# Neighbourhood attention in blocks of 8 columns on quarters of the matrix array, with a joined first load and a residual that waits in PSUM

## The chip, the cores and the metric

One core of one Trainium2 chip runs the whole layer. The metric is the device time of one execution in microseconds, as the median of several runs. The core has a matrix engine (TensorE, PE in the profile; its weight loads are PEld), a vector engine (VectorE, DVE), a scalar engine (ScalarE, ACT), GpSimd (POOL) and SyncE (SP), which here issues transfers. A suffix q (SPq, ACTq) marks an engine's queue of instructions that are not work of its own, such as issues of transfers.

## The reference, cut to what matters

One encoder layer in float32 on 512 tokens (8 rows of 64 columns) of 2048 features:

```python
xn = rms_norm(x, attn_norm_g)
u_val, u_gate, q, k, v = split(xn @ w_in)          # 1024 columns each
y_conv = silu(layer_norm(depthwise_conv31(u_val * sigmoid(u_gate))))
y_na = neighborhood_attention(q, k, v, rpb)        # 16 heads of 64
x = x + concat(rms_norm(y_conv), rms_norm(y_na)) @ w_out
up = depthwise_conv3(rms_norm(x) @ w_up)           # 2 x 5632 columns
gate, val = split(up)
x = x + (silu(gate) * val) @ w_down
out = rms_norm(x)

# neighborhood_attention, for the token in grid row r, grid column c:
#   the window is all 8 grid rows, and 16 grid columns from
#   clip(c - 8, 0, 48);  p = softmax(q.k / 8 + bias[head, dr, dc]);  out = p.v
```

With 8 grid rows the window takes in every row, so that only the columns limit it: a query in column c sees keys of 16 columns about c.

## The kernel before

**Numbers.** Large products are made of two or three matmuls of a reduced float32 type (fp32r): an operand is split into a high part, rounded by ScalarE (`whi`, `xh`), and a low remainder, by VectorE (`wlo`, `xl`). `group` multiplies a 128x1024 unit of weights in this way: 8 high weights with the high and the low activations (L153, L154), then 8 low weights with the high ones (L156), 24 matmuls of 512 columns. Attention alone, and the transposes, work in plain float32.

**Stages.** 16 steps in the order `ORDER = "aaaqqaqaaaqqaqqq"` make the input projection: a step "a" is a gate and a value projection of 128 convolution channels (`glu`, two projections), a step "q" is q, k and v of a pair of heads (`qkv`, three projections). A projection is two units. Then the output projection in two halves, the up projection (44 blocks of seven products, a fast matrix multiplication of two by two blocks with seven products), the down projection of the same kind (`product2`, seven products of 22 units), and the last norm. TensorE's order is that of the program as the tile framework schedules it by priorities; `pin` keeps a group of instructions in program order.

**Attention between the projections.** After each unit, `tick` takes one step of the first generator in `steps`, with its instructions placed behind the unit just multiplied. `attend` is such a generator: loads of the bias tables, then the turned values and the scores with their softmax, three or four ticks of pause, then the transposes of the probabilities (`turn`, L521) with their copies out of PSUM (`turned_p`, L529), then the values (`values`, L538) with their copy (L571) into the split operand of the output projection.

The 64 grid columns are cut into 4 blocks of 16 columns; a block is 128 queries (8 rows x 16 columns). The two edge blocks have 192 keys, the two middle blocks 256, in groups of 8 columns (64 keys). A score matmul (L495) has 64 rows of the array, the features of one head, and 128 columns, the queries; the two heads of a pair lie on the two halves of the rows. For keys that do not start at an even group, `qkv` makes a second copy `ks` of the keys on ScalarE with the groups exchanged in pairs, and `turned_v` arranges the turned values twice (`edge`, `vt`, five copies on ScalarE). A value matmul has 128 keys on the rows and the 64 features of one head on half of the columns, and moves 128 queries; the two heads lie on the two halves of the columns. PSUM tiles: `sc` (two banks) holds edge scores and later edge transposes, two `tr` banks the middle ones, `po` (one bank) the turned values and later the result of the values. Two statistics of the convolution's norms (`root_steps`, the matmul `st<-dg` L255) use `sc` as well.

**The start.** `w_0` holds the weights of the first gate and the first value projection, interleaved by the 16 rows of 128 features. The first rows come as separate loads: the norm's scales `g1` and three weight pieces on ScalarE's queue, x on SyncE's. `first_glu` multiplies a row of x with two weight blocks as soon as it is there: six matmuls a row (L369, L373). 11 matmuls of ones (`WARM`, L124) run ahead of it. The next projections follow with whole units.

**The end.** The last product, `product2(5, a, False)`, starts four PSUM banks anew; its last four units are multiplied bank by bank (`TAIL`), so that each bank's end can be worked on beside the next. In `ready` VectorE adds the bank to the partial sum `x` of the other products (L935), ScalarE squares that with a sum (L937), VectorE multiplies with the last norm's gain (L939, or together with the scale, L965, for the last block of a row); `write` makes the scale of the norm from the sums, multiplies and stores (L953 to L969), the last block of a row first.

Of the kernel before, what the change touches and what calls it, by code (L numbers as in the profile page):

```python
# [16 lines left out]
P = 128  # L17
# [19 lines left out]
BLK = 16  # L37
NB = GW // BLK
HG = 8
EDGE, MID = (0, 3), (1, 2)  # L40
KEYS = ((0, 0, 3 * DH), (1, 0, 4 * DH), (1, 2 * DH, 4 * DH), (0, 5 * DH, 3 * DH))
ATEDGE = ((0, 0), (1, 1)), ((1, 2), (2, 3))
ATMID = ((0, 0), (1, 1)), ((2, 1), (3, 2))
# [8 lines left out]
WARM = 11  # L52
# [26 lines left out]
def layer(ctx: ExitStack, tc: tile.TileContext, xT, xn, w_0, w_in, w_out, w_up, w_down, par, tab, g3, out):  # L79
# [26 lines left out]
    nc.scalar.dma_start(g1, par[:, :KD])  # L106
    cuts = (0, 1, 2, 4, 8, 12, 16)
    first = []
    for k0, k1 in zip(cuts[:3], cuts[1:4]):
        first.append(t2("we")[:, :2 * (k1 - k0) * P])  # L110
        nc.scalar.dma_start(first[-1], w_0[:, 2 * k0 * P:2 * k1 * P])
# [159 lines left out]
    def split_x(k, x):  # L271
        h, l = t2("xh", F32R), t2("xl", F32R)
        pin(nc.scalar.activation(h, x, AF.Copy, scale=g1[:, k:k + 1]))
        pin(nc.vector.scalar_tensor_tensor(l, x, g1[:, k:k + 1], h.bitcast(F32), op0=ALU.mult, op1=ALU.subtract))
        xs.append((h, l))

    def piece(raw, k0, k1):
        if k1 - k0 > 2:
            raw, i = raw_unit(w_0[:, 2 * k0 * P:2 * k1 * P], 2 * (k1 - k0) * P)
            pin(i)  # L280
            w = parts(raw, 2 * (k1 - k0) * P)
        else:
            w = t2("weh", F32R)[:, :2 * (k1 - k0) * P], t2("wel", F32R)[:, :2 * (k1 - k0) * P]
            w += nc.scalar.activation(w[0], raw, AF.Copy), nc.vector.tensor_sub(w[1], raw, w[0].bitcast(F32))
        pin(w[2])
        pin(w[3])
        return k0, k1, w[0], w[1]

    pieces, early = [], []
    for k in range(2):  # L290
        x = t2("x")
        pin(nc.sync.dma_start(x, xT[0][:, k * S:(k + 1) * S]))
        split_x(k, x)
        pieces.append(piece(first[k], k, k + 1))
    for p, at in ((1, 2), (2, 3), (3, 0), (4, 4), (5, 0), (6, 5), (7, 0)):
# [4 lines left out]
        if at:  # L300
            pieces.append(piece(first[2] if at == 2 else None, cuts[at], cuts[at + 1]))
    squares = sm.tile([P, S // P, 2], F32, tag="ss", name="ss")
    for u in range(2):
        raw, i = raw_unit(w_in[NC_ + 1, :, u * U * P:(u + 1) * U * P], U * P)
        pin(i)
        for t in range(2 * u, 2 * u + 2):
            for i in range(2):
                x = t4([P, D // 2], "xn")
                pin(nc.sync.dma_start(x, xn[t * P:(t + 1) * P, i * D // 2:(i + 1) * D // 2]))
                if t == 2 * u and i == 0:  # L310
                    w = parts(raw, U * P)
                    pin(w[2])
                    pin(w[3])
                    early.append(w[:2])
                pin(nc.scalar.activation(x, x, AF.Square, accum_out=squares[:, t, i:i + 1]))
    last = pin(nc.sync.dma_start(prm, par))
    for i in range(6):
        plan.append(lambda i=i: early[i - 4] if i > 3 else None)
# [6 lines left out]
    del plan[6:12]  # L325
# [5 lines left out]
    def stats1():  # L331
        for _ in range(3):
            yield
# [19 lines left out]
    ys, ypair = [], []  # L353

    def glu(i):
        pg, pv = project(NC_ + i), project(i)

        late.append(lambda: gated(i, pg, pv))

    def first_glu():  # L360
        two = [psa.tile([P, S], F32, tag="tr", name="pj", bufs=2) for _ in range(2)]
        for n, (k0, k1, hi, lo) in enumerate(pieces):
            if n > 1:
                weights()
            for k in range(k0, k1):
                for x in range(2):
                    for i, ps in enumerate(two):
                        o = (2 * (k - k0) + i) * P
                        nc.tensor.matmul(ps, hi[:, o:o + P], xs[k][x], start=k == x == 0, stop=False)  # L369
            for k in range(k0, k1):  # L370
                for i, ps in enumerate(two):
                    o = (2 * (k - k0) + i) * P
                    m = nc.tensor.matmul(ps, lo[:, o:o + P], xs[k][0], start=False, stop=k == KD - 1)  # L373
            if n > 1:
                tick(m)
        late.append(lambda: gated(0, *two))
# [63 lines left out]
    def grid(t, c0, w):  # L440
        return t.rearrange("p (r c) -> p r c", c=GW)[:, :, c0:c0 + w]

    def qkv(p):
        got = []
        for j, nm in enumerate("qkv"):
            ps = project(2 * NC_ + j * NP_ + p)
            if nm == "q":

                t = t2(nm)
                by = "p (r b c) -> p r b c"  # L450
                nc.vector.tensor_mul(t.rearrange("p (b r c) -> p r b c", b=NB, r=WH),
                                     ps.rearrange(by, b=NB, r=WH), rstd[0].rearrange(by, b=NB, r=WH))
            else:

                t = t2(nm)
                by = "p (r g c) -> p r g c"
                nc.vector.tensor_mul(t.rearrange("p (g r c) -> p r g c", g=2 * NB, r=WH),
# [620 lines left out]
```

## Time and profile before

| | |
|---|---|
| median of 3 runs | 1969.95 us (1969.86 to 1970.58) |
| profiled execution, its own time | 1970.17 us |
| its span in the profile | 1968.4 us |
| busy: TensorE, weight loads, VectorE, ScalarE, GpSimd | 1956.4, 1665.2, 1608.1, 1100.9, 225.3 us |
| transfers | 447.83 MB, 228 GB/s over the span |

A row of a timeline is: start in us, length in us, engine, line, operation, destination<-sources by tile names, shapes, number of instructions merged into the row, and in brackets how long the engine was idle before it and what released it. A row of waits is: engine, tile and line that waited, what it waited for, us in total, times, longest. Lengths of matmul records include their latency, so that records overlap; the pace is the distance from start to start.

### The profile page before, as it was taken

What the parts mean: (1) busy time and instruction counts of PE and PEld (TensorE: products, weight loads), DVE (VectorE), ACT (ScalarE), POOL (GpSimd) and SP (SyncE); (2) the same over time, 40 slices, a digit from 0 to 9 for tenths busy, and PEclk for the clock granted to TensorE, in tenths of its full rate; (3) what the DMA queues carried; (4) which work ended last, traced back from release to release, by engine and by line L of the source; (5) the groups of instructions that cost most, each with busy time, mean ns of one, the idle gap of its engine ahead of it and who ended that gap; (6) DMA issues with size and microseconds to landing.
All of it is one profiled execution on the core that took longest, in us unless ns stands there. A gap on an engine that the chain in (4) does not pass through costs nothing.

```text
span 1968.4 us, 27634 instructions
## 1 busy us (share of the span) xinstructions
PE 1956.4 (99%) x10125; PEld 1665.2 (85%) x10125; DVE 1608.1 (82%) x2339; ACT 1100.9 (56%) x1766; POOL 225.3 (11%) x310
## 2 busy tenths in 40 slices
PE   9999999999999999999999999999999999999998
PEld 7888888888888888888888888888888888888886
DVE  5987687798557889898989898888888898885765
ACT  6244424448526666666666666666666644554654
POOL 0111111111001111111111111111110400000000
PEclk9999999999999999999999999999999999999999
DMA  9776766676858899999999999999986977666563
GB/s 363 182 196 173 187 178 185 179 190 203 258 147 213 206 251 244 271 246 272 236 274 245 268 242 269 242 270 246 265 229 168 387 242 233 217 214 193 192 201 120
DMA packets 141817, 447.83 MB, mean 228 GB/s; under 512 B 15088, under 2 KB 27632, under 8 KB 140272
## 3 DMA queue, kind: packets, MB, share of 16 engines
q1 hardware_dynamic: 88880, 290.31, 43.4%
q0 software_dynamic: 42624, 148.92, 35.3%
q10 hardware_dynamic: 10176, 6.83, 1.1%
q8 instruction: 80, 1.31, 0.3%
q14 instruction: 57, 0.47, 0.1%
HBM read 427.12 MB, written 111.15 MB: 273 GB/s over the span
## 4 chain that ended last, share of the span: by engine, by line
PE 98%; DVE 1%; DMA 0%; issue 0%; ACT 0%; ACTq 0%; DVEq 0%
PE pu L745 44%; PE pd L884 21%; PE pj L153 7%; PE pj L154 7%; PE pj L156 7%; PE po L153 3%; PE po L154 3%; PE po L156 3%; PE po L538 1%; PE sc L495 1%; PE pj L369 1%; PE trp L521 1%; DMA we<-in_w 0%; PE trx L640 0%; PE pj L373 0%
## 5 line engine op out<-in xcount | busy, mean ns | idle before, releaser
L136 ACT ACTIVATE whi<-raw 128x1024 fp32r<-128x1024 f32 x573 | 605.0, 1057 | 543.3 <-PE pj L154 154.7
L137 DVE TENSOR_TENSOR wlo<-raw,whi 128x1024 fp32r<-128x1024 f32 x573 | 699.3, 1221 | 235.4 <-ACT whi L136 196.3
L745 PE MATMUL pu<-xc,whi 128*128 128x512 f32 x2464 | 593.6, 391 | 0.0
L745 PEld LDWEIGHTS pu<-xc,whi 128*128 128x128 f32 x2464 | 451.3, 188 | 86.7 <-DVE xc L633 0.4
L745 PEld LDWEIGHTS pu<-xc,wlo 128*128 128x128 f32 x2464 | 319.2, 191 | 13.7
L745 PE MATMUL pu<-xc,wlo 128*128 128x256 f32 x2464 | 324.2, 283 | 0.0
L884 PE MATMUL pd<-whi,ho 128*128 128x512 f32 x1232 | 305.1, 389 | 0.1
L884 PEld LDWEIGHTS pd<-whi,ho 128*128 128x128 f32 x1232 | 231.1, 188 | 48.7 <-DVE vl L758 0.5
L153 PE MATMUL pj<-xh,whi 128*128 128x512 f32 x608 | 238.9, 393 | 0.0
L154 PE MATMUL pj<-xl,whi 128*128 128x512 f32 x608 | 236.8, 389 | 0.0
L395 DVE SCALAR_TENSOR_TENSOR y<-ch,prm,y 128x500 f32<-128x500 f32 (+14 forms) x240 | 177.2, 742 | 5.3
L884 PE MATMUL pd<-wlo,ho 128*128 128x512 f32 x616 | 165.1, 389 | 0.0
L156 PE MATMUL pj<-xh,wlo 128*128 128x512 f32 x608 | 150.3, 389 | 0.0
L153 PEld LDWEIGHTS pj<-xh,whi 128*128 128x128 f32 x608 | 114.1, 188 | 26.7 <-issue 2.8
L884 PEld LDWEIGHTS pd<-wlo,ho 128*128 128x128 f32 x616 | 115.6, 188 | 24.0
L156 PEld LDWEIGHTS pj<-xh,wlo 128*128 128x128 f32 x608 | 114.1, 188 | 23.7
L154 PEld LDWEIGHTS pj<-xl,whi 128*128 128x128 f32 x608 | 114.2, 188 | 23.5 <-issue 0.2
L754 ACT ACTIVATE pu<-pu 128x512 f32<-128x512 f32 x132 | 76.5, 580 | 92.9 <-PE pu L745 92.8
L694 POOL DMA_DIRECT2D raw<-in_w_up x88 | 78.0, 887 | 366.1 <-DVE wlo L137 143.9
L208 POOL DMA_DIRECT2D ws<-in_w_down x88 | 79.5, 903 | 301.5 <-DMA ws<-in_w_down 126.6
L205 POOL DMA_DIRECT2D ws<-ws x44 | 23.0, 524 | 317.9 <-PE pj L156 105.1
L205 POOL DMA_DIRECT2D ws<-in_w_down x44 | 23.2, 528 | 306.9 <-PE pj L156 174.5
(193 smaller groups left out, 1967.8 us busy)
## 6 DMA issues: line engine op xcount, KB each, us to landing
raw<-in_w_up SPq DMA_DIRECT2D x220, 512.0 KB, 5.9
ws<-in_w_down POOLq DMA_DIRECT2D x132, 512.0 KB, 6.3
raw<-in_w_up POOLq DMA_DIRECT2D x88, 512.0 KB, 7.3
raw<-ws SPq DMA_DIRECT2D x88, 512.0 KB, 3.6
raw<-in_w_in SPq DMA_DIRECT2D x76, 512.0 KB, 5.2
raw<-in_w_down SPq DMA_DIRECT2D x66, 512.0 KB, 4.1
ws<-ws POOLq DMA_DIRECT2D x44, 512.0 KB, 5.8
raw<-in_w_out SPq DMA_DIRECT2D x32, 512.0 KB, 4.7
```

Source lines behind the costliest of these rows:

```text
L136: i = nc.scalar.activation(hi[:, :n], raw[:, :n], AF.Copy)
L137: j = nc.vector.tensor_sub(lo[:, :n], raw[:, :n], hi[:, :n].bitcast(F32))
L153: nc.tensor.matmul(ps, hi, mh, start=first and k == 0, stop=False)
L154: nc.tensor.matmul(ps, hi, ml, start=False, stop=False)
L156: i = nc.tensor.matmul(ps, lo[:, wk * P:(wk + 1) * P], mh, start=False, stop=last and k == len(ws) - 1)
L205: behind(nc.gpsimd.dma_start(wsum[c][k], a), ins)
L208: nc.gpsimd.dma_start(wsum[c][k], w_down[k, {1: A21, 2: A11, 4: A11, 6: A12}[c]], accum_op=ALU.add, max_dma_last_dim=ROW)
L395: nc.vector.scalar_tensor_tensor(y[:, a:b], h[:, a + j - PAD:b + j - PAD], prm[:, o:o + 1], y[:, a:b], op0=ALU.mult, op1=ALU.add)
L694: nc.gpsimd.dma_start(a[c], w_up[f, q2], accum_op=ALU.add)
L745: i = nc.tensor.matmul(ps[:, :n], part[:, k * P:(k + 1) * P], comb[c][k][:, :n], start=j == 0 and not more, stop=j == 2 * U - 1, skip_grou ...
L754: nc.scalar.activation(to, ps, AF.Copy)
L884: m = nc.tensor.matmul(ps[i], h[:, o + t * P:o + (t + 1) * P], w[:, d], start=start and not more and kind == 0 and j == 0, stop=stop and k ...
```

## The change

Three parts are changed at once.

*Attention.* The 64 grid columns are cut into 8 blocks of 8 columns, each 64 queries, with 192 keys: its own group of 8 columns and one on each side. The blocks stand in two `QUADS`; of a quad, two blocks (one odd, one even) share the upper 64 partitions and two the lower 64, so that a softmax works on 128 partitions x 2 x 192. A score matmul has 64 rows (the features of a head) and 64 columns (the queries of a block); the table of the six slots of 64 keys is so laid out that each pair of slots begins with an even key group after the transposes: 12 transposes for a pair of heads, where there were 14. A value matmul has 64 keys on the rows (even groups on the upper half, odd groups on the lower half) and 64 features on the columns, and writes up to three blocks at once; even and odd key groups are summed in two banks (`sc`), in the order of `TURNS`, and VectorE adds the second bank to ScalarE's copy of the first. The second copy of the keys and the double turned values are gone; a table is 768 instead of 640 columns.

*The start.* The first gate, the first value and the second gate projection are multiplied together, nine matmuls for a row of x. For the first four rows (`ROWS`) x and its weights come in one load each (`xw`; the first one carries the scales too), all on SyncE's queue; the first row's split is shared out between ScalarE and VectorE. The loads for the sums of squares are moved between those of later rows. `WARM` is 8. The second gate stays in its bank until `glu(1)` takes it, and the first gated values are made right behind the first product, not after the next unit.

*The end.* Before the last product, ScalarE copies the partial sums into its four PSUM banks (`prime`, in the ticks of the product before); the product adds to them. `ready` squares and multiplies straight from PSUM, and the addition is gone there. `write` stores the blocks of a row in ascending order.

```diff
+HG = 8
+NB = GW // HG
+QUADS = ((1, 2), (3, 4)), ((5, 6), (7, 0))
+SLOTS = 3 * DH
+TURNS = (((0, 1, 5, 1, 0), (1, 1, 5, 1, 0)), ((0, 0, 0, 1, 1), (1, 0, 0, 2, 1)), ((2, 0, 1, 3, 1), (3, 0, 2, 3, 2)),
+         ((4, 0, 4, 2, 3), (5, 1, 0, 2, 5)), ((4, 1, 0, 1, 5), (5, 0, 5, 1, 4)), ((6, 1, 1, 3, 5), (7, 1, 2, 2, 6)))
-WARM = 11
+WARM = 8
+ROWS = 4
...
+    for k in range(ROWS):
+        n = 3 * P
+        both = t4([P, S + n + KD], "xw")
+        m = S + n + (0 if k else KD)
+        pin(nc.sync.dma_start(both[:, :m], xw[k][:, :m]))
...
+            his = [t2("weh", F32R)[:, :P], t2("weh", F32R)[:, P:n]]
+            h, l = t2("xh", F32R), t2("xl", F32R)
+            g = both[:, S + n:S + n + 1]
+            pin(nc.scalar.activation(h[:, :H], x[:, :H], AF.Copy, scale=g))
+            pin(nc.vector.tensor_copy(his[0], raw[:, :P]))
+            pin(nc.vector.tensor_scalar(h[:, H:], x[:, H:], g, None, op0=ALU.mult))
+            pin(nc.scalar.activation(his[1], raw[:, P:], AF.Copy))
...
     def first_glu():
-        two = [psa.tile([P, S], F32, tag="tr", name="pj", bufs=2) for _ in range(2)]
+        three = [psa.tile([P, S], F32, tag="tr", name="pj", bufs=2) for _ in range(2)]
+        three.append(psm.tile([P, S], F32, tag="mm", name="pj"))
...
-        late.append(lambda: gated(0, *two))
+        gate.append(three[2])
+        gated(0, *three[:2])
...
+        def scores(quad, both):
+            todo = [[], []]
+            for i, (odd, even) in enumerate(quad):
+                if even:
+                    todo[i] += [(odd, 0, odd - 1, 3), (even, 3, even - 1, 3)]
+                else:
+                    todo[i] += [(odd, 0, odd - 1, 2), (odd, 2, 0, 2), (even, 4, even, 2)]
+            order = [(1, 0), (1, 1), (0, 0), (0, 1)] if len(todo[1]) > 2 else [(0, 0), (1, 0), (0, 1), (1, 1)]
+            order += [(1, 2)] * (len(todo[1]) > 2)
+            for i, n in order:
+                b, to, g, w = todo[i][n]
                 for j, hp in enumerate(hps):
+                    m = nc.tensor.matmul(both[j][hps[i], to * DH:(to + w) * DH], q[hp, b * DH:(b + 1) * DH],
+                                         k[hp, g * DH:(g + w) * DH], start=True, stop=True)
...
+        def values(po):
+            for n, slot in enumerate(TURNS):
+                for i, (g, quad, at, w, b) in enumerate(slot):
                     for j in (1, 0):
+                        m = nc.tensor.matmul(po[i][hps[j], b * DH:(b + w) * DH], vt[0][hps[i], g // 2, hps[j]],
+                                             pts[2 * quad + j][hps[i], at * DH:(at + w) * DH],
+                                             start=n == 0, stop=n == len(TURNS) - 1, skip_group_check=True)
...
-        po = psa.tile([P, S], F32, tag="po", name="po")
-        values(po, EDGE, pts[:2], ATEDGE)
-        values(po, MID, pts[2:], ATMID, True)
+        two = psa.tile([P, 2, S], F32, tag="sc", name="po")
+        po = [two[:, i] for i in range(2)]
+        values(po)
         ao = t2("ao")
-        nc.scalar.activation(ao, po, AF.Copy)
+        nc.scalar.activation(grid(ao), po[0].rearrange("p (g r c) -> p g r c", g=NB, r=WH), AF.Copy)
+        nc.vector.tensor_add(grid(ao), grid(ao), po[1].rearrange("p (g r c) -> p g r c", g=NB, r=WH))
...
-            add(x[i], x[i], ps[i])
+            if not whole:
+                add(x[i], x[i], ps[i])
+            src = ps[i] if whole else x[i]
             q = t2("sq")
-            nc.scalar.activation(q, x[i], AF.Square, accum_out=sq[th][:, t, o:o + 1])
+            nc.scalar.activation(q, src, AF.Square, accum_out=sq[th][:, t, o:o + 1])
...
+    def prime(x):
+        primed.extend(four(True))
+        for a, b in zip(x, primed):
+            nc.scalar.activation(b, a, AF.Copy)
             yield
...
-        for d in reversed(range(Q)):
+        for d in range(Q):
...
-    steps += [ready(e0, a, 0, 1), ready(e1, a, 1, 1)]
+    steps += [ready(e0, a, 0, 1), ready(e1, a, 1, 1), prime(e3)]
...
-    a = four(True)
-    for i in product2(5, a, False):
+    for i in product2(5, primed, True):
```

More of the change, by code (lines that the diff above doesn't have):

```diff
@@ L296, in layer @@
+    for p in range(ROWS // 2, KD // 2):
         x = t4([P, 2 * S], "x")
@@ L331, in stats1 @@
     def stats1():
-        for _ in range(3):
+        for _ in range(2):
             yield
```

259 lines of the change are left out of this document (113 added, 146 removed).

## The prediction, made before the changed kernel ran

> **What bounds the kernel now.** I read the page's first and fourth parts, then the list of waits of TensorE, then the timeline at the three places that the change touches.
>
> ```profile
> span 1968.4 us, 27634 instructions
> PE 1956.4 (99%) x10125; PEld 1665.2 (85%) x10125; DVE 1608.1 (82%) x2339; ACT 1100.9 (56%) x1766; POOL 225.3 (11%) x310
> ...
> PE 98%; DVE 1%; DMA 0%; issue 0%; ACT 0%; ACTq 0%; DVEq 0%
> ...
> PE pj L369 <- ACT weh L284: 1.8, 2, 1.3
> PE warm L124 <- DVE ones L119: 1.1, 1, 1.1
> PE st L264 <- DVE acc L226: 0.2, 1, 0.2
> ```
>
> TensorE is busy for 1956.4 of 1968.4 us, and 98% of the chain that ended last is its own. The last three rows are all its waits on others: two in the first microseconds, and one of 0.2 us in the rest. So only three things change the time: less TensorE work, an earlier start of its unbroken stream, a shorter tail behind its last matmul. Vector and scalar work beside the stream is free as long as no new wait appears. The profiled execution took 1970.17 us (1.77 us around its span), 0.22 us above the median of 1969.95; I work out a difference against it and take it from the median.
>
> **The pace of TensorE in attention.** The rows are the timeline of the first pair of heads (scores, transposes, values, each with the projection matmul behind it), a narrow window at the first two value matmuls, and the durations of single records (min/median/max). Each of these fp32 matmuls stands as two records, two passes; a transpose stands as one.
>
> ```profile
> 118.26 0.92 PE L495 MATMUL sc<-k,q 64*128 64x192 f32 x8
> 119.01 1.03 PE L495 MATMUL sc<-ks,q 64*128 64x256 f32 x8
> 119.97 0.50 PE L153 MATMUL pj<-xh,whi 128*128 128x512 f32 x1
> ...
> 136.43 1.69 PE L521 MATMUL trp<-ident,s 128*128 128x128 f32 x14
> 137.87 0.48 PE L153 MATMUL pj<-xh,whi 128*128 128x512 f32 x1
> ...
> 143.54 1.09 PE L538 MATMUL po<-pt,edge 128*64 128x128 f32 x16
> 144.46 1.04 PE L538 MATMUL po<-pt,vt 128*64 128x128 f32 x16
> 145.44 0.50 PE L153 MATMUL pj<-xh,whi 128*128 128x512 f32 x1
> ...
> 143.54 0.33 PE L538 MATMUL po<-pt,edge 128*64 128x128 f32 x2
> ...
> L495 PE MATMUL sc<-k,q x64: 322/323/427, 118.3 to 513.7; 64*128 64x192 f32 x64
> L495 PE MATMUL sc<-ks,q x64: 376/376/376, 119.0 to 514.5; 64*128 64x256 f32 x64
> L538 PE MATMUL po<-pt,edge x128: 272/273/323, 143.5 to 539.2; 128*64 128x128 f32 x128
> ```
>
> 64 more columns make a record 53 ns longer (376 less 323), so a pass streams 0.83 ns per column: 0.160 us for 192 columns, 0.213 for 256, 0.107 for 128, 0.053 for 64. The transposes agree: 14 between 136.43 and 137.87 are 0.103 each. But 32 value records between 143.54 and 145.44 are only 0.059 each, half a pass. So two run at once, one for each half of the array's columns; the row with x2 shows it, two records of 0.32 us in 0.33 us together. Scores likewise: eight passes of each width, in pairs, are 4 x 0.160 + 4 x 0.213 = 1.49 of the 1.71 us between 118.26 and 119.97, and the other 0.22 is filling and leaving the mode. Values: 16 x 0.107 = 1.71 of 1.90, with 0.19 over.
>
> **Attention after the change.** A matmul now uses 64 rows and 64 columns, a quarter of the array, and four can be in flight. Scores of a pair of heads: each quarter gets 4 x 192 columns (in one of them partly as three of 128), in two passes 8 x 0.160 = 1.28 us, with the same 0.22 over 1.50 where 1.71 was: -0.21. Transposes: 12 for 14, -2 x 0.103 = -0.21. Values: six slots, the widest entry of each 64, 128, 192, 128, 64 and 192 columns, 768 in all, two passes 1.28 us, with 0.19 over 1.47 where 1.90 was: -0.43. Sum -0.85 a pair, times 8 pairs -6.8 us, all of it on the path, since TensorE never waits there. If quarters run ahead of each other, the longest queue of the value slots is 704 columns and 0.11 goes too, -7.7 in all, and with a shorter fill of narrower weights about -8.3. If the queue is strictly in order, the three-part quarter of the second score group holds the others up for at most one entry, 2 x 0.107: -5.1.
>
> Four at once is not in the trace; two at once is, in both directions (two halves of rows in the scores, two of columns in the values), each at full pace. I take four as the product of both. The Trainium skill says the same on its page "TensorEngine Tiling (Array Packing)", Key Properties: different tiles load weights and multiply in parallel; no run here shows it for four.
>
> **What it moves on other engines.** Per pair ScalarE loses two key copies and four of five copies of the turned values, VectorE gains one addition out of PSUM (0.68 us, the addition at 1959.91 below) and works 4 x 384 score columns where it had 2 x 384 and 2 x 512. Cover: the softmax has the same three to four units of projection to finish, and the list of waits has none of TensorE on it. SyncE's queue carries as many table loads, of 786 instead of 655 KB a pair; the weights behind them are fetched four ahead. Where the cover goes: values now land in the two banks that scores and turned probabilities use too. In the order of the built program one statistics matmul (the second of the convolution's norm) stands 7 matmuls behind the values of the sixth pair and needs these banks, so it waits for the copy and the new addition. In the trace of before that place looks like this:
>
> ```profile
> 455.56 0.73 PE L255 MATMUL st<-dg,ones 128*128 128x512 f32 x2
> ...
> 455.67 0.60 ACT L571 ACTIVATE ao<-po 128x512 f32<-128x512 f32 x1 [2.61 <-PE po L538]
> ```
>
> The copy ends 0.7 us behind the values, the addition 0.7 us later at best, 1.4 in all, and 7 matmuls of 0.22 cover 1.6; with VectorE late by an instruction or two the wait is 0 to 1.5 us. TensorE and everything on it stands behind it. I take +0.5, once.
>
> **The start.** Rows: the timeline up to 11.03 us, landings of first loads (KB, us from issue), and transfer rates (last column, GB/s) of two stretches.
>
> ```profile
> 1.06 5.06 PE L124 MATMUL warm<-ones 128*128 128x128 f32 x22 [1.06 <-DVE ones L119]
> 5.14 0.42 ACT L284 ACTIVATE weh<-we 128x256 fp32r<-128x256 f32 x1 [0.15 <-DMA we<-in_w]
> 5.78 0.82 PE L369 MATMUL pj<-xh,weh 128*128 128x512 f32 x2
> 8.40 0.42 ACT L284 ACTIVATE weh<-we 128x256 fp32r<-128x256 f32 x1 [2.23 <-DMA we<-in_w]
> 8.87 0.73 PE L369 MATMUL pj<-xh,weh 128*128 128x512 f32 x2 [1.34 <-ACT weh L284]
> 11.03 0.50 PE L369 MATMUL pj<-xh,weh 128*128 128x512 f32 x1 [0.50 <-ACT weh L284]
> ...
> x<-in_xT SPq DMA_DIRECT2D x2, 256.0 KB, 3.5
> we<-in_w ACTq DMA_DIRECT2D x2, 128.0 KB, 5.3
> ...
> 0.00:3.80 3.80, 2.74 (x13) 1.00 0.46 128
> 14.00:34.00 20.00, 20.00 (x90) 1.00 1.02 397
> 60.00:80.00 20.00, 20.00 (x90) 1.00 0.85 228
> ```
>
> Before, six matmuls run at 5.78, six at 8.87, and the stream is unbroken from 11.03; both gaps end with a weight piece that shared the rings with rows of x. At the steady pace (90 in 20 us, 0.222 us; 0.229 here) the twelve are 2.75 us, so the stream starts in effect at 8.28. Afterwards one load brings x, three weight blocks and the scales of row 0: 467 KB, alone at the head of its queue. 128 GB/s over the first 3.8 us is 486 KB, so it is moved by about 3.8 and usable at about 4.2 (the 256 KB that shared the rings took 3.5 from issue at 0.75). One conversion of 0.42 behind it puts the first matmul at 4.7; eight warming matmuls, 16 passes of 0.23, end there too. The warm passes are 0.23 apart where a transpose pass is 0.103, so TensorE starts at half pace; in the old start the full pace is there soon after 6. Three or four first matmuls cost 0.2 each too much, and the stream starts in effect at 5.4 to 5.5: -2.8 us. From then a row of x is nine matmuls, 2.06 us, against 459 KB, 1.16 us at 397 GB/s, and further on two rows with their weights and a block of squares, 1.43 MB, 3.6 us, against 4.1 us: TensorE isn't starved. Bounds: at -3.6 the row comes half a microsecond earlier and warm; at 0 a later gap eats it.
>
> **The end.** Timeline:
>
> ```profile
> 1958.42 1.32 ACT L963 ACTIVATE xr<-xr,rsy 128x512 f32<-128x512 f32 x2
> 1958.56 1.07 PE L884 MATMUL pd<-wlo,ho 128*128 128x512 f32 x4
> 1959.91 0.68 DVE L935 TENSOR_TENSOR xr<-xr,pd 128x512 f32<-128x512 f32 x1
> 1960.62 0.63 ACT L937 ACTIVATE sq<-xr 128x512 f32<-128x512 f32 x1 [0.88 <-DVE xr L935]
> 1963.15 0.95 ACTq L969 DMA_DIRECT2D out_T<-xr  x2
> ```
>
> TensorE ends at 1959.63; the addition waits for VectorE until 1959.91, and the square follows at 1960.62. With the residual already in PSUM the square reads the bank as soon as ScalarE is free, 1959.74: -0.9 us. What follows is the same chain; the two halves of a row change order. Priming is four copies of about 0.6 us on ScalarE in the ticks of the product before the last, 12 ticks of 22, hidden there. Bounds -1.2 (the additions in the middle delay the last one no more) and -0.4 (the final scaling reads PSUM and gives some back).
>
> **Sum.** -6.8 + 0.5 - 2.8 - 0.9 = -10.0: 1960.2 against 1970.17, 1960.0 against the median. With all favourable ends 1956.8, with the unfavourable ones (-5.1, +1.5, -1.0, -0.4) 1965.0.
>
> **Rivals.** *Two at a time.* Four quarters could run no better than two: rows and columns may pair only one way. Then scores stream 2.56 us and values, 1408 columns in two passes, 2.34: with the overheads 2.78 and 2.53 for 1.71 and 1.90, less 0.21, +1.49 a pair, +11.9; with the rest +8.7, 1978.6, slower. It decides where fewer than 2.9 run at a time (9.8 us of serial streaming per pair against 3.4), and below about 2.6 it makes the whole slower. For it: no row shows four. Against: both pairings run at full pace. 11%.
>
> *Starts bind.* 64 passes and 64 weight loads in 3.20 us are 25 ns for each instruction; if that is a limit and no coincidence, 84 and 84 need 4.2: +0.79 a pair with the transposes, +6.3, in all 1973.1, no change. If only matmul starts count, just the 64-column rounds suffer (four starts, 0.10 for 0.053; four rounds a pair): 1961.5. Against: in the row with x2 the second record starts within 0.01 us of the first. 4% for the first kind; the second kind lies inside the range. The Trainium skill has such a floor ("TensorE: Matmul & The Clock Gate", section on 56 ns against 53.3: starts never closer than about 25 ns); the trace disagrees for matmuls on different tiles.
>
> *The start gains nothing*, because a load late in the first 38 us opens a gap of the same size: -7.2 instead of -10.0, 1962.8. For it: the transfers run at their limit there. Against: 3.6 us against 4.1. 10%.
>
> **How the numbers follow.** The forecast has 75%. The range 1956.8 to 1965.0 takes in its bounds and the third rival and leaves out the first and the slow kind of the second, 15%. A measurement of this kernel tells apart about 0.2%, 3.9 us: faster 0.85 (forecast and third), same 0.04, slower 0.11.
>
> **What would show it.** Right: four score records with starts within 0.03 us, scores 1.5 and values 1.5 us up to the next projection matmul, 12 transposes 1.24, first real matmul near 4.7 with no wait behind it, square within 0.2 us of the last matmul, TensorE busy about 1949. Wrong: records in pairs, scores at 2.8; a row in the waits of TensorE on the additions out of the value banks by more than 1.5; a wait on a weight piece between 12 and 40 us.

## The result and the profile after

| | before | after |
|---|---|---|
| median (lowest to highest), us | 1969.93 (1969.86 to 1970.58) | 1960.05 (1959.87 to 1961.08) |
| profiled execution, us | 1970.17 | 1960.14 |
| its span, us | 1968.4 | 1958.4 |
| last matmul ends, us of the span | 1959.63 | 1950.00 |
| from there to the end of the span, us | 8.8 | 8.4 |

The ratio of after to before is 0.9951, with a 95% interval of 0.9939 to 0.9962: faster by 9.9 us. The forecast was 1960.0 us. It came out almost exactly, but partly because errors of its terms cancel, which is what most of this document is about.

The page of after (span, engines, the chain) and the list of waits of TensorE, whose last columns are total, times and longest in us:

```profile
span 1958.4 us, 28132 instructions
PE 1948.2 (99%) x10391; PEld 1657.4 (85%) x10391; DVE 1605.9 (82%) x2348; ACT 1084.3 (55%) x1724; POOL 225.8 (12%) x310
...
PE 99%; DVE 1%; issue 0%; ACT 0%; DVEq 0%
...
PE warm L118 <- DVE ones L113: 1.1, 1, 1.1
PE st L431 <- DVE acc L428: 0.6, 1, 0.6
```

TensorE has 266 records more and is busy 8.2 us less. The two waits on weight pieces in the first microseconds (1.8 us) are gone. So is the wait of 0.2 us of the kernel before, which stood at the sums of squares of the convolution's norm (`st<-ones,acc`, in the trace of before):

```profile
447.13 1.02 PE L264 MATMUL st<-ones,acc 128*128 128x1 f32 x8 [0.20 <-DVE acc L226]
```

A new wait of 0.6 us stands at another matmul, the first statistics matmul of that norm, on the additions over channels (`st<-acc`; both tiles are called `acc`). TensorE still is 99% of the chain.

The timeline of after at the first pair of heads, as shown of before (the first row is the answer for a window of 0.1 us at the first scores):

```profile
115.03 0.39 PE L497 MATMUL sc<-k,q 64*64 64x192 f32 x4
...
115.03 1.59 PE L497 MATMUL sc<-k,q 64*64 64x192 f32 x36
116.55 0.50 PE L147 MATMUL pj<-xh,whi 128*128 128x512 f32 x1
...
133.01 1.47 PE L522 MATMUL trp<-ident,s 128*128 128x128 f32 x12
134.24 0.48 PE L147 MATMUL pj<-xh,whi 128*128 128x512 f32 x1
...
139.91 1.44 PE L538 MATMUL po<-pt,vt 64*64 64x64 f32 x48
141.28 0.50 PE L147 MATMUL pj<-xh,whi 128*128 128x512 f32 x1
```

Four score records are done 0.39 us after the first one starts, and one alone has up to 0.374 us: four are in flight, with their starts within 0.02 us. From the first start to the next projection matmul the scores have 1.52 us (1.71 before), the transposes 1.23 (1.44), the values 1.37 (1.90). All eight pairs look alike.

The timeline of after at the start:

```profile
1.06 3.78 PE L118 MATMUL warm<-ones 128*128 128x128 f32 x16 [1.06 <-DVE ones L113]
4.17 0.51 ACT L304 ACTIVATE xh<-xw 128x256 fp32r<-128x256 f32 x1 [1.93 <-DMA xw<-in_xw]
4.80 1.21 PE L386 MATMUL pj<-xh,weh 128*128 128x512 f32 x3
5.85 0.86 PE L386 MATMUL pj<-xl,weh 128*128 128x512 f32 x3
6.55 0.85 PE L390 MATMUL pj<-xh,wel 128*128 128x512 f32 x3
```

and the landing of its first load (KB, us from its issue at 0.75 us):

```profile
xw<-in_xw SPq DMA_DIRECT2D x1, 456.0 KB, 3.4
```

The joined row is usable at 4.17 us, the first real matmul starts at 4.80, and from 5.85 on there is one each 0.23 us, without a gap.

The timeline of after at the end:

```profile
1948.93 1.07 PE L888 MATMUL pd<-wlo,ho 128*128 128x512 f32 x4
1950.05 0.60 ACT L943 ACTIVATE sq<-pd 128x512 f32<-128x512 f32 x1 [0.41 <-PE pd L888]
1953.16 0.34 ACTq L983 DMA_DIRECT2D out_T<-xr  x1
```

and the landing of this last store (the same columns as for the load), in after and then in the kernel before, where it is issued at 1963.77:

```profile
out_T<-xr ACTq DMA_DIRECT2D x1, 256.0 KB, 4.1
```

```profile
out_T<-xr ACTq DMA_DIRECT2D x1, 256.0 KB, 3.5
```

The square follows the last matmul by 0.05 us (0.99 before), and the last store is issued 3.16 us behind it (4.14 before). But this store lands 4.1 us after its issue instead of 3.5, which takes back 0.6 of the 1.0 us.

### The profile page after: what moved, and what is told of

It is laid out like the page before. It is cut to its first block, busy times and chain, and to the rows that moved or that the text cites. A ratio compares the mean times of both kernels' runs of the same rounds, so it can differ in the third digit from the quotient of the medians.

```text
span 1958.4 us, 28132 instructions
## 1 busy us (share of the span) xinstructions
PE 1948.2 (99%) x10391; PEld 1657.4 (85%) x10391; DVE 1605.9 (82%) x2348; ACT 1084.3 (55%) x1724; POOL 225.8 (12%) x310
## 3 DMA queue, kind: packets, MB, share of 16 engines
q10 hardware_dynamic: 9600, 6.29, 1.1%
## 4 chain that ended last, share of the span: by engine, by line
PE 99%; DVE 1%; issue 0%; ACT 0%; DVEq 0%
PE pu L749 44%; PE pd L888 21%; PE pj L147 7%; PE pj L148 7%; PE pj L150 7%; PE po L147 3%; PE po L148 3%; PE po L150 3%; PE pj L386 1%; PE po L538 1%; PE pj L390 1%; PE sc L497 1%; PE trp L522 1%; PE trx L644 0%; DVE acc L428 0%
## 5 line engine op out<-in xcount | busy, mean ns | idle before, releaser
L130 ACT ACTIVATE whi<-raw 128x1024 fp32r<-128x1024 f32 (+1 forms) x574 | 604.3, 1054 | 535.8 <-PE pj L148 134.6
L131 DVE TENSOR_TENSOR wlo<-raw,whi 128x1024 fp32r<-128x1024 f32 (+1 forms) x574 | 698.9, 1218 | 221.4 <-ACT whi L130 194.1
L147 PE MATMUL pj<-xh,whi 128*128 128x512 f32 x592 | 233.2, 394 | 0.0
L148 PE MATMUL pj<-xl,whi 128*128 128x512 f32 x592 | 230.8, 390 | 0.0
L150 PE MATMUL pj<-xh,wlo 128*128 128x512 f32 x592 | 146.2, 389 | 0.0
```

The source lines that it names most:

```text
L130: i = nc.scalar.activation(hi[:, :n], raw[:, :n], AF.Copy)
L131: j = nc.vector.tensor_sub(lo[:, :n], raw[:, :n], hi[:, :n].bitcast(F32))
L147: nc.tensor.matmul(ps, hi, mh, start=first and k == 0, stop=False)
L148: nc.tensor.matmul(ps, hi, ml, start=False, stop=False)
L150: i = nc.tensor.matmul(ps, lo[:, wk * P:(wk + 1) * P], mh, start=False, stop=last and k == len(ws) - 1)
```

## The experiments

### The three parts alone

Each kernel has one part of the change on the kernel before. The core line of each part:

```diff
 # attn_only
-                    m = nc.tensor.matmul(both[j][:, i, :], q[hp, b * P:(b + 1) * P], ks[swapped][hp, at:at + w],
+                    m = nc.tensor.matmul(both[j][hps[i], to * DH:(to + w) * DH], q[hp, b * DH:(b + 1) * DH],
 # start_only
+        pin(nc.sync.dma_start(both[:, :m], xw[k][:, :m]))
 # end_only
-    for i in product2(5, a, False):
+    for i in product2(5, primed, True):
```

> The kernel before with the attention part of the change alone. Theory (the three parts add up, attention is matmul time on the path): scores 1.714 to 1.525, values 1.898 to 1.374, transposes 1.446 to 1.227 us a pair, 8 x 0.93 = -7.5 us, less a wait of up to 0.7 us on a statistics matmul: 1962.5 to 1963.2. Rival (attention gives most back in new waits, the gain is that of start and end): within 2 us of the kernel before, 1968 or more.

> The kernel before with the new start alone. Theory: the first real matmul comes 1.0 us earlier and gaps of 2.3 us behind it go, nothing is given back later: 1966.5 to 1967.0, no wait on a weight piece. Rival (a load late in the first 40 us opens a gap of the same size, or the sums of squares come late): 1969 or more, with a row for it in the waits of TensorE.

> The kernel before with the primed last product alone. Theory: the last square starts 0.9 us earlier and the last store is issued 0.9 to 1.0 us earlier; the stores' landings and the waits for them at the very end give up to 0.6 of it back: 1969.0 to 1969.6. Rival (what gave it back in the changed kernel was a straggling store in that one execution): 1968.9 to 1969.1, the whole 0.9.

| kernel | median (range), us | less than before (1969.92) | last matmul, us | from there to the span's end, us |
|---|---|---|---|---|
| attn_only | 1963.31 (1963.13 to 1963.85) | 6.6 | 1953.31 | 8.8 |
| start_only | 1968.16 (1967.55 to 1968.40) | 1.8 | 1956.62 | 9.3 |
| end_only | 1968.87 (1968.33 to 1969.59) | 1.1 | 1959.11 | 7.6 |

The ratios are 0.9966 (0.9954 to 0.9979), 0.9990 (0.9981 to 0.9999) and 0.9995 (0.9986 to 1.0004); the last interval takes in 1, so that the gain of the end alone is not clear of noise. The parts sum to 9.4 us; together they give 9.9. Attention is two thirds of the gain. The start is the surprise: TensorE ends 3.0 us earlier with it, but 1.2 us of that is missing from the median. In its profiled execution 0.6 us of it was lost behind the last matmul, in code that this kernel didn't touch. The other 0.6 us is chance: the profiled execution of before was 0.2 us above its median, that of start_only (1967.72) 0.4 us below. Here is the last store's landing in start_only:

```profile
out_T<-xr ACTq DMA_DIRECT2D x1, 256.0 KB, 4.1
```

So 4.1 us instead of 3.5 comes with the start, not with the new end. (The runs of start_only fell into two groups, near 1967.6 and 1968.3; why is not known.)

### Do the quarters run ahead of each other?

The matmuls of after in another order: scores of a group sorted by the half of the columns that they use, values first all of the even key groups, then all of the odd ones.

```diff
-            for i, n in order:
+            for i, n in sorted(order):
...
-            for n, slot in enumerate(TURNS):
-                for i, (g, quad, at, w, b) in enumerate(slot):
+            for i in range(2):
+                for n, slot in enumerate(TURNS):
+                    g, quad, at, w, b = slot[i]
```

> The changed kernel with the same matmuls in another order: all scores of the blocks on one half of the columns ahead of those on the other, and all values of even key groups ahead of those of odd ones, so that only two neighbours in program order lie on different quarters. Theory A (matmuls start in program order; a quarter is free for later ones only when the queue has got to them): two at a time, scores 2.8 us and values 2.5 us a pair, +2.35 x 8 = +18.8, about 1979. Theory B (each quarter takes its matmuls out of the queue on its own, far ahead): no change, 1960.

Measured: 1966.49 us (1966.25 to 1967.45), ratio 0.9983 (0.9974 to 0.9992), 6.4 us above after. Its timeline at the values of the first pair:

```profile
139.65 2.27 PE L539 MATMUL po<-pt,vt 64*64 64x64 f32 x48
141.85 0.50 PE L147 MATMUL pj<-xh,whi 128*128 128x512 f32 x1
```

The values have 2.20 us instead of 1.37, 0.83 x 8 = 6.6 us, which is the whole loss; the scores are unchanged at 1.52. Two at a time would have needed 2.53, so that part of the second half still ran beside the first. Neither theory holds as it stood. A quarter does go on while the next matmuls in order wait for a busy one, since the sorted scores, up to four matmuls in a row for two quarters, lost nothing; but not past twelve such matmuls. The look-ahead is limited, and the limit lies between these.

### The wait on `acc`

In the changed kernel TensorE waits 0.6 us at the first statistics matmul of the convolution's norm (`st<-acc`). The timeline of after there, VectorE and then TensorE:

```profile
421.02 0.68 DVE L428 TENSOR_TENSOR acc<-acc,y 128x512 f32<-128x512 f32 x1
421.62 1.22 DVE L131 TENSOR_TENSOR wlo<-raw,whi 128x1024 fp32r<-128x1024 f32 x1
422.76 0.68 DVE L428 TENSOR_TENSOR acc<-acc,y 128x512 f32<-128x512 f32 x1
424.14 2.12 DVE L428 TENSOR_TENSOR acc<-acc,y 128x512 f32<-128x512 f32 x3
...
426.41 1.10 PE L431 MATMUL st<-acc,ones 128*128 128x512 f32 x2 [0.58 <-DVE acc L428]
```

Seven additions must be done before the matmul, and VectorE has a split of weights of 1.22 us (421.62) between them. In the kernel before, the split stood behind the last four of them:

```profile
430.38 2.85 DVE L410 TENSOR_TENSOR acc<-acc,y 128x512 f32<-128x512 f32 x4
433.14 2.35 DVE L137 TENSOR_TENSOR wlo<-raw,whi 128x1024 fp32r<-128x1024 f32 x2
```

This wait comes with the attention part: attn_only has it too (0.6 us), start_only and end_only don't. Three kernels try to take the wait away.

**One unit later.** The matmul is moved behind one more unit of projection:

```diff
             nc.vector.tensor_add(acc, acc, ys[i])
         yield
+        yield
         ps = psa.tile([P, 2, S], F32, tag="sc", name="st")[:, 0]
```

> The changed kernel, with the first statistics matmul of the convolution's norm one unit of projection later. Theory A: TensorE's only wait in the stream, 0.6 us at that matmul, comes from VectorE's order (one split of weights of 1.22 us stands between the additions that the matmul needs), so one unit later it is gone: 1959.4 us against 1960.05, and no row of TensorE on `acc`. Theory B: the wait belongs to the banks that scores, turned probabilities and values share, and only moves: 1960.0 us, with a wait of about 0.5 us at another statistics matmul.

Measured: 1967.85 us (1966.58 to 1968.16), ratio 0.9987 (0.9979 to 0.9996): 7.8 us slower. Its two longest waits of TensorE behind the first microseconds, from the list:

```profile
PE po L147 <- DVE oa L623: 4.2, 1, 4.2
...
PE st L249 <- DVE dg L245: 1.0, 2, 0.7
```

and its timeline behind the longest one:

```profile
504.52 0.79 PE L147 MATMUL po<-mah,whi 128*128 128x512 f32 x1 [4.23 <-DVE oa L623]
505.11 0.63 PE L148 MATMUL po<-mal,whi 128*128 128x512 f32 x1
...
508.52 0.59 PE L148 MATMUL po<-mal,whi 128*128 128x512 f32 x1
508.95 0.40 PE L147 MATMUL po<-mah,whi 128*128 128x512 f32 x1
```

The wait on `acc` is gone, as theory A said, but neither theory has the time: everything behind it in this chain of steps is one unit later too, and at its end the output projection waits 4.2 us for its first operand. Then TensorE runs at half its pace: ten matmuls from 504.52 to 508.95 take 0.43 us each instead of 0.23, 2 us more. The granted clock is 0.50 there (from 505 to 508 us).

**Two additions on GpSimd.**

```diff
+        some = t2("some")
+        nc.gpsimd.tensor_add(some, ys[0], ys[1])
+        nc.gpsimd.tensor_add(some, some, ys[2])
-        nc.vector.tensor_add(acc, ys[0], ys[1])
-        for i in range(2, NC_):
-            nc.vector.tensor_add(acc, acc, ys[i])
+        nc.vector.tensor_add(acc, ys[3], ys[4])
+        nc.vector.tensor_add(acc, acc, ys[5])
+        for y in (ys[6], some, ys[7]):
+            nc.vector.tensor_add(acc, acc, y)
```

> The changed kernel; of the seven additions over channels ahead of the first statistics matmul of the convolution's norm, two run on GpSimd, which adds up the first three channels beside VectorE's work; nothing moves on TensorE. Theory A: the wait of 0.6 us at this matmul comes from VectorE being late there (about 0.7 us an addition, and a split of weights of 1.22 us between them); with two additions less it is 1.4 us earlier, the wait is gone, and the time is 0.6 us less: 1959.45 against 1960.05 us. Theory B: TensorE is held there by the bank or by the additions' data whatever VectorE does (GpSimd may also be slower than 1.5 us an addition); the wait stays at 0.6 us or grows, 1960.0 us or more.

Measured: 1961.94 us (1961.14 to 1962.98), ratio 0.9959 (0.9946 to 0.9971), 1.9 us slower than after. The timeline of this kernel, GpSimd, VectorE and the wait:

```profile
412.89 1.58 POOL L427 TENSOR_TENSOR some<-y 128x512 f32<-128x512 f32 x1
414.55 2.17 POOL L428 TENSOR_TENSOR some<-some,y 128x512 f32<-128x512 f32 x1
412.59 2.98 DVE L131 TENSOR_TENSOR wlo<-raw,whi 128x1024 fp32r<-128x1024 f32 x1 [1.23 <-PE pj L150]
415.49 2.54 DVE L413 SCALAR_TENSOR_TENSOR y<-ch,prm,y 128x499 f32<-128x499 f32 x2
427.57 2.05 PE L435 MATMUL st<-acc,ones 128*128 128x512 f32 x2 [1.99 <-DVE acc L432]
```

and of after at the same place:

```profile
412.83 1.22 DVE L131 TENSOR_TENSOR wlo<-raw,whi 128x1024 fp32r<-128x1024 f32 x1 [1.24 <-PE pj L150]
413.98 1.50 DVE L413 SCALAR_TENSOR_TENSOR y<-ch,prm,y 128x499 f32<-128x499 f32 x2
```

While GpSimd adds, VectorE's split takes 2.98 us instead of 1.22, and two taps 2.54 instead of 1.50: 2.8 us lost to save two additions, 1.4 us. VectorE is 1.4 us later in all, and the wait grows by just this, from 0.6 to 2.0 us. The fix failed, but it moves the cause by a known amount, and the wait follows. The Trainium skill, on its page "SBUF — State Buffer", section on the two separate sides, has VectorE and GpSimd share a pair of ports as an exclusive lock, also where a VectorE instruction has two operands in SBUF; the split has two such operands, and these rows agree that the two engines slow each other; which of them held the ports when, they don't show.

**Five additions some 40 us earlier** (from 378.4 us on), on VectorE, when the last channel begins; on the kernel with the tables split (next section):

```diff
+        if i == NC_ - 1:
+            acc = t2("acc")
+            nc.vector.tensor_add(acc, ys[0], ys[1])
+            for n in range(2, NC_ - 2):
+                nc.vector.tensor_add(acc, acc, ys[n])
+            first_sum.append(acc)
...
-        acc = t2("acc")
-        nc.vector.tensor_add(acc, ys[0], ys[1])
-        for i in range(2, NC_):
+        acc = first_sum[0]
+        for i in range(NC_ - 2, NC_):
             nc.vector.tensor_add(acc, acc, ys[i])
```

> The changed kernel with the table loads issued as two each, and with five of the seven additions over channels ahead of the first statistics matmul put some 60 us earlier on VectorE, beside the taps of the last channel; the order of TensorE is the same, and GpSimd has no share in it. Theory A: VectorE's lateness alone makes the wait of 0.6 us; the last addition now stands ahead of the split of weights that it stood behind, so the wait is gone: 0.6 us less than with the tables split alone, 1959.25 against 1959.86 us. Theory B: the wait is set by something else at this place (the last tap of the last channel, the bank): it stays at 0.4 us or more, 1959.7 to 1959.9 us.

Measured: 1959.21 us (1958.92 to 1959.64), ratio 0.9945 (0.9932 to 0.9959), where 1959.25 was expected. The list of its waits of TensorE, all of it:

```profile
PE warm L118 <- DVE ones L113: 1.1, 1, 1.1
PE pj L386 <- ACT weh L299: 0.2, 1, 0.2
```

and its timeline of VectorE:

```profile
420.25 0.68 DVE L435 TENSOR_TENSOR acc<-acc,y 128x512 f32<-128x512 f32 x1
...
421.70 1.22 DVE L131 TENSOR_TENSOR wlo<-raw,whi 128x1024 fp32r<-128x1024 f32 x1 [0.25 <-ACT whi L130]
```

The last addition ends at 420.93, ahead of the split, and the wait is gone. VectorE's lateness was the cause. That it was this one split is argued from its length and place, since five additions were moved too. No run of this kernel is as slow as the fastest of the changed kernel (1959.87); against the tables split alone its median is 0.65 us lower, and the ranges overlap a little (from 1959.39).

### Where the end's gain went

In the trace of after, one packet of 8 KB of instructions is fetched 6.11 us behind the last matmul, amid the last packets of the stores, and the landing behind it is the last, at 7.28 us; the others have ended by 6.86. In the kernel before this fetch comes at 8.43 us, when all has landed. Its place goes with SyncE's instructions: it stands behind 1237 of SyncE's records in before, attn_only and end_only, and behind 1234, or 1233 in the kernel with the matmul one unit later, in the seven kernels with the new start and whole tables.

**Tables split.** 16 issues of transfers more in SyncE's stream, with packets of the same size:

```diff
-            i = nc.sync.dma_start(tb, tab[2 * p:2 * p + 2, :, n * 2 * SLOTS:(n + 1) * 2 * SLOTS]
-                                  .rearrange("h p k -> p h k"))
+            for j in range(2):
+                i = nc.sync.dma_start(tb[:, j], tab[2 * p + j, :, n * 2 * SLOTS:(n + 1) * 2 * SLOTS])
```

> The changed kernel, with each load of a bias table issued as two (one for each head): the same bytes in packets of the same size, 16 more instructions in SyncE's stream. Theory A: the last store lands late because a piece of SyncE's own instructions (8 KB) is fetched amid the last stores (it starts 6.11 us behind the last matmul, and the landing behind it comes at 7.28 us, where the others have ended by 6.86); with more instructions ahead the fetch comes before the stores, the last landing comes at about 6.9 us, and the time falls by 0.4 us to 1959.65. Theory B: the stores are late for another reason, such as where the output lies in memory; the fetch moves and the last landing stays at 7.2 to 7.3 us, 1960.05.

Measured: 1959.86 us (1959.39 to 1960.37), ratio 0.9948 (0.9934 to 0.9961). The row of its last store:

```profile
out_T<-xr ACTq DMA_DIRECT2D x1, 256.0 KB, 3.6
```

No fetch is left in the tail, and the last store lands after 3.6 us, not 4.1; from the last matmul to the span's end it is 7.8 us instead of 8.4. The last landing is at 6.71 us behind the last matmul, and at 6.70 and 6.72 in the two other kernels with split tables. With the fetch at 6.02 to 6.12 us it came at 7.19 to 7.30 in four kernels (after, halves, one_warm, sum_on_gpsimd). So in the profiles the late landing goes with the fetch. It does not strike each time: in the kernel with the matmul one unit later the fetch came at the same place, 6.10 us, and the last landing was in time, at 6.84. The median moved by 0.2 us only, and the ranges overlap, so that the gain in time is not shown clear of noise, and its price is not settled better than 0.2 to 0.5.

**Other memory.** The new end alone, with the inputs of the new start in memory:

```diff
+    pin(nc.sync.dma_start(consts.tile([P, KD], F32, name="spare"), xw[0][:, -KD:]))
...
+    w_0 = np.ascontiguousarray(np.concatenate([w_0, w_3[:, :KD * P]], axis=1))
-    arrays = {"xT": xT, "xn": np.ascontiguousarray(a["x"][0]), "w_0": w_0, "w_in": w_in,
+    arrays = {"xT": xT, "xn": np.ascontiguousarray(a["x"][0]), "xw": np.ascontiguousarray(xw), "w_0": w_0, "w_in": w_in,
```

> Only the new end on the kernel before, with the new start's inputs in memory (the joined rows as one more input, the first weights with three blocks a row instead of two), of which only one small load is used. Theory A: the longer packets of the last stores in all kernels with the new start (the longest 200 ns, where 164 ns are the longest without it) come from where the output lies in memory; then they are long here too, and the time is 0.3 us above the new end alone: 1969.2 against 1968.87 us. Theory B: they come from the fetch of instructions and from what is issued beside it; then packets stay at 120 to 165 ns, and the time is 1968.9 us.

Measured: 1969.19 us (1968.86 to 1969.39), ratio 0.9995 (0.9986 to 1.0004). The last store's row in end_only, and then in this kernel:

```profile
out_T<-xr ACTq DMA_DIRECT2D x1, 256.0 KB, 3.3
```

```profile
out_T<-xr ACTq DMA_DIRECT2D x1, 256.0 KB, 4.0
```

The long packets are here with the old start (the longest 281 ns, 164 in end_only), and the last data are written 0.23 us later (6.29 us behind the last matmul, 6.06 in end_only). This points at the place in memory as a second cause, beside the start's instructions, but does not show it: in this kernel fetches also fell at 1.99 and 6.46 us, the second ahead of the last landing at 7.10, so that the two shares aren't apart; and the medians differ by 0.32 us, within their ranges.

**Descending stores.** The order of the last pieces as in the kernel before:

```diff
-        for d in range(Q):
+        for d in reversed(range(Q)):
```

> The changed kernel, with the pieces of the last row block scaled and stored from the last to the first again, as in the kernel before. Theory A: the order takes part in the end's gain (the end alone moved the last landing by 1.26 us, of which the square's place explains 0.94), because the piece that waits in PSUM is then scaled first and the last store is issued about 0.2 to 0.3 us later: 1960.3 us. Theory B: the order does nothing, 1960.05 us.

Measured: 1960.33 us (1959.97 to 1961.06), ratio 0.9951 (0.9938 to 0.9965). In its profiled execution the span behind the last matmul is 8.39 us against 8.37: no effect of the order is seen. The median is 0.28 us up, where theory A had it, but inside the range of after; not settled, and small.

**Both small edits.** The additions on GpSimd, and the tables split:

> Both of the last small edits together, on the changed kernel: two additions on GpSimd, and each table load issued as two, which takes the fetch of SyncE's instructions out of the last stores. If the two causes are separate, the gains add: 0.6 us from the wait and 0.2 to 0.5 us from the tail, 1959.0 to 1959.3 us. If the wait is not what costs, 1959.8 us as with the tables alone.

Measured: 1961.42 us (1960.38 to 1961.85), ratio 0.9956 (0.9943 to 0.9968). The wait on `acc` is 1.8 us, as GpSimd makes it, and the last landing is in time at 6.70 us. The median is 0.5 us below that with GpSimd alone, as if the tail's gain added, though the ranges overlap; but neither number that was expected came, because the GpSimd edit costs.

### What the warm matmuls buy

```diff
-WARM = 8
+WARM = 1
```

> The changed kernel with one warming matmul instead of eight. Theory A: TensorE runs at half pace for its first microseconds of work, whatever the work is; then the first real matmuls from 4.8 us on have 0.4 us each instead of 0.22 for about 3 us of work, some 8 of them, and the time is 1.2 to 1.7 us longer, 1961.2 to 1961.8 us. Theory B: the first stretch is bound by the arrival and conversion of data alone; 1960.05 us.

Measured: 1962.11 us (1961.60 to 1963.04), ratio 0.9960 (0.9946 to 0.9973): 2.1 us slower, more than expected. Its timeline:

```profile
4.83 1.62 PE L386 MATMUL pj<-xh,weh 128*128 128x512 f32 x3 [2.98 <-DVE g L308]
6.25 1.48 PE L386 MATMUL pj<-xl,weh 128*128 128x512 f32 x3
...
10.09 1.27 PE L386 MATMUL pj<-xl,weh 128*128 128x512 f32 x3
11.20 0.86 PE L390 MATMUL pj<-xh,wel 128*128 128x512 f32 x3
```

The data come as early as in after, but three matmuls take 1.28 us until about 11 us, and 0.7 after that: about 14 matmuls at half pace. Theory A holds; the half pace lasted 6 us of work, not 3.

## Why the prediction was right, step by step

| step | forecast, us | in the profiled executions, us |
|---|---|---|
| scores, 8 pairs | -1.7 | -1.5 |
| transposes | -1.7 | -1.8 |
| values | -3.4 | -4.2 |
| a new wait | +0.5 | +0.4 (a new one of 0.6, the old one of 0.2 gone) |
| start | -2.8 | -3.2 (first scores, 115.03 for 118.26; -3.0 in start_only) |
| end | -0.9 | -0.4 |
| sum | -10.0 | -10.7, of -10.0 in all |

Of the 0.7 us between the last two numbers some 0.3 lie about the sixth pair, where statistics matmuls that stood right behind the transposes and the values now stand between projection matmuls. The rest is spread over TensorE's stream, and I cannot attribute it.

- **Four at a time** is right. The rival with two at a time falls with the score rows: it needed 2.78 us for the scores, and they have 1.52. The Trainium skill's statement that tiles load and multiply in parallel ("TensorEngine Tiling (Array Packing)", Key Properties) holds here for four. *Starts bind* falls too: four starts lie within 0.02 us, so that the 25 ns that the skill gives between starts ("TensorE: Matmul & The Clock Gate", section on 56 ns against 53.3) do not hold between matmuls on different quarters. That rival was also counted wrong: scores and values of before have 48 passes in 3.20 us, not 64 (16 and 32 a pair), 33 ns for each instruction with the weight loads. After has 84 in the 2.89 us of its scores and values, 17 ns.
- **The values** were the mis-sized term. I took 768 columns, six slots in step with each other, for 1.47 us; they have 1.37, which is what the 704 columns of the longest queue give (1.17 us and 0.19 over). The bound was the better value, and that needs quarters that run ahead; halves shows that they do, within a limit. For the scores I kept the same 0.22 us over; here it is 0.24.
- **The wait** had the right size at the wrong place. I looked for it at the second norm's statistics (`st<-dg`), behind the values in their new banks; the list of waits has nothing there, since the 7 matmuls cover it (the addition ends at 449.04, the matmul starts at 449.31). It is at `st<-acc`, through the order of VectorE's instructions. The failed step: I followed who needs the banks, and said that vector work beside the stream is free as long as no new wait appears, but did not read in the built order which VectorE instructions had moved ahead of which.
- **The start** is right in its times (4.17 against 4.2, 4.80 against 4.7) and too small by 0.2 to 0.4, in part since I charged three or four matmuls at half pace: in after's profiled execution only the first ran so (0.56 us to the next), while others had two to three (start_only), four to five (descending_stores) and five to six (later). The term is not a constant of the kernel. The old start isn't one either: its waits on weight pieces are 1.8 us in before, 1.4 in attn_only and 0.9 in end_only.
- **The end** is right up to the last issue of a store (0.98 us earlier, 0.9 forecast) and wrong behind it. "What follows is the same chain" is the sentence that failed: the landing of the last store went from 3.5 to 4.1 us. With the fetch out of the way it is 3.6. Without the new start the new end takes 1.2 us off the tail (7.6 for 8.8 in end_only), more than forecast. That the new start costs at the other end of the kernel, through the count of SyncE's instructions and perhaps through memory, was in none of my rivals.

So the forecast's 1960.0 rests on a sum in which 1.4 us more from the values, the start, the transposes and the wait stand against 1.4 us less from the end, the scores and the unexplained rest. Its sign, its size and its main mechanism are shown; that it fell within 0.1 us is luck.

## What to carry to other kernels

Small matmuls pay per quarter of the array: give each of the four quarters the same number of columns in total, and mix them in the order of issue, since a quarter goes on past a busy one only so far (four matmuls in a row cost nothing here, twelve did). Where TensorE is never idle, read the other engines' built order at each place where it needs them: a single vector instruction that slips in ahead can make TensorE wait (here one of 1.22 us, 0.6 us), and moving a whole chain of steps later, or sharing the work with GpSimd, can cost several times more than the wait. A tail of stores can be held up by transfers that the change does not name: compare the time from issue to landing there, not only the issues.

## What the runs showed of the hardware

- **Half pace after idling.** After a pause of 4.2 us in the middle of the kernel, TensorE ran at 0.43 us a matmul for 4.4 us; at the start, with one warm matmul, for 6 us. The Trainium skill ("TensorE: Matmul & The Clock Gate", Part 1) gives a budget of about 3.4 us of time that varies from run to run; these runs agree that it varies (4.4 and 6 us here), and it was longer than 3.4 us in both; whether it counts time or matmuls they don't show.
- **Look-ahead between quarters.** Up to four matmuls in a row for two of the quarters cost nothing; twelve in a row cost 0.83 us of 2.20.
- **Instruction fetches stand amid the stores.** They have queues of their own (q14, where the stores have q1 and q10), and 8 KB took 0.31 us at the end of after. With one amid the last store's packets this store landed up to 0.5 us later, though not each time.
- **GpSimd slows VectorE.** Beside two GpSimd additions (3.75 us), 2.7 us of VectorE work took 5.5 us.
